# A two-layer trunk with a mixture of experts: conditioning's last four loads summed on PE, slots' weights taken from the transposed slot matrix, overflow tests at other pairs

## The chip, the cores and the metric

The kernel runs on one core of one Trainium2 chip. The metric is device time in microseconds (us) from start to end, as the median of several runs; beside it stands one execution with the hardware profiler, from which all rows are taken. Engines are named as in the profile: PE (TensorE) with its weight loads (PEld), DVE (VectorE), ACT (ScalarE), POOL (GpSimd), SP (SyncE, which only issues transfers here).

## What is computed

Two layers on 256 tokens with D = 1024, all in float32. A layer conditions its input with scale and shift vectors made from one vector c, mixes tokens by three branches (retention, attention with forget gates, latent attention) that are merged by gates and projected, then conditions again and runs a mixture of 32 experts: top-1 of four groups, then the two best experts of that group.

```python
for l in range(DEPTH):
    mod = silu(c) @ ada_w[l] + ada_b[l]              # 6 vectors of 1024: shift, scale, gate, twice
    h = modulate(rms_norm(x, norm1_g[l]), sh1, sc1)
    x = x + g1 * token_mixer(h, positions, ...)
    h = modulate(rms_norm(x, norm2_g[l]), sh2, sc2)
    x = x + g2 * hier_moe(h, ...)
return rms_norm(x, final_norm_g)

def hier_moe(h, w_grp, b_grp, w_exp, b_exp, w1, w3, w2):
    grp_p = softmax(t @ w_grp + b_grp);  g_idx = argmax(grp_p);  g_w = max(grp_p)
    exp_logits = (t @ w_exp + b_exp).reshape(T, 4, 8)
    top_p, top_i = top_k(softmax(exp_logits of g_idx), 2)
    wts = g_w[:, None] * top_p / sum(top_p)
    # each token goes to its two experts e with its weight w:
    y += w * ((silu(xb @ w1[e]) * (xb @ w3[e])) @ w2[e])
```

## The kernel before

**Tiles and stages.** Tokens are two tiles of 128 partitions (NT = 2); x stays on chip. A layer is `mixer(l)` and then `moe(l)`. Weights come from HBM as loads of 1 MiB (128 partitions, 2048 floats). `Ring.plan` lists all loads in the order in which they are wanted, and `Ring.fill` (L139) issues them in that order, all from SP, each as soon as a slot is free and its data may be overwritten. There are 12 slots of their own; in the MoE seven or so more places join, in tiles named `more_right`, `more_left` and `ar`. SP's queue goes in order: a load that waits for its slot holds up all loads behind it.

**Conditioning.** `ada()` takes loads of `ada_w`, two halves for each vector part. A load of a part in `vec` is summed by DVE in four operations (L511) into `acc`, and PE adds the sum of the partitions (`add_up` with `cz`). Any other load is summed by PE itself: four matmuls, each with 32 rows of output. `ga` is the generator that does one load per `next`; it is interleaved with the mixer. The last `ADA_TAIL` loads of a layer are planned behind the loads of the output projection. `ADA_FIRST` of them are taken in front of `route()`, any others in the MoE.

**From the mixer to the MoE.** `out()` multiplies by `out_w` in two halves of 512 columns, n = 0 and 1. After each half `residual` (L592, L593 on DVE, L594 on ACT, squares) updates x, and `router_half(n)` transposes x on PE (L188), copies the transposes by ACT (L1224) and multiplies them by the router's weights (matmuls with 36 columns). Then `route()` forms the inverse rms and runs `choose()` for both tiles, a chain of small DVE operations with, here and there, a `pulse`: one PE matmul on the operation's result, which nothing reads. It leaves `rr` (each token's place among its expert's tokens) and `W` (its weight) for each expert, both in the tile `rt`.

**The MoE.** The experts go in 16 pairs, numbered 0 to 15. An expert has CAP = 64 slots for tokens, so a pair has 128. For pair p: `up` of w1 into the bank G[0] (32 matmuls); `combine(p - 1)` adds the last pair's result to the tokens' sums (with OT, the transposed one-hots); silu on ACT (L1415); `slots_of(p)`; `up` of w3 into G[1]; the gather of the next pair's tokens (matmuls of x with one-hots made by DVE); hid transposed; w2; and the weighted results as two parts yh (L1454, ACT) and yl (L1455, DVE), scaled by `wsl`, the weight of each slot.

`slots_of(p)` makes one-hots on DVE (L1318), transposes them on PE, gets `wsl` by two matmuls of the one-hots with two columns of W, and copies both out of the bank:

```python
self.mm(ps[:, 256:258], oh[t], self.W[:, t, 2 * p:2 * p + 2], t == 0, t == 1)
...
nc.vector.tensor_copy(wsl(p)[es], ps[es, 256 + e:257 + e])        # L1372
nc.vector.tensor_copy(self.OT, ps[:, 0:256])                      # L1373
```

In front of pair OVERFLOW = 12 stands `overflow(l)`: a branch on whether any expert has more than 64 tokens (the rows show it not taken). `final_gain`, two matmuls and copies that spread the last norm's gain, stands at pairs 11 and 12 of the last layer.

Of the kernel before, what the change touches and what calls it, by code (L numbers as in the profile page):

```python
# [14 lines left out]
ALU = mybir.AluOpType  # L15
AX = mybir.AxisListType
# [4 lines left out]
NT = 2  # L21
DEPTH = 2
D_IN = 3524
NE = 32
CAP = 64
# [20 lines left out]
A_END = 9216  # L46


ADA_TAIL, ADA_FIRST = 2, 2

ADA_BEHIND = {2048: 1, 2560: 1, 0: 1}

# [4 lines left out]
WAIT_MLA, WAIT_FOX, WAIT_RET, WAIT_PT = 4, 4, 2, 1  # L57
SLOTS = 12

OVERFLOW = 12  # L60


def table(inputs):
# [102 lines left out]
class Trunk:  # L166
# [771 lines left out]
    def run(self, gen):  # L938
        for _ in gen:
            self.step(self.live)  # L940
# [84 lines left out]
    def mixer(self, l):  # L1025
        nc, run, finish = self.nc, self.run, self.finish
# [16 lines left out]
        def chain():  # L1043
            self.rowsA = yield from self.ada(l, 4, range(6), space, self.R, range(6))
            yield from self.gs(l, 1, 12 * l + 6, self.rowsA)
            yield from self.router_terms(l)
            while not self.y_free and gr not in self.live:
                yield
            yield from self.gate_rows(12 * l + 4, A_GT1, self.rowsA)
            self.gated = True  # L1050
            yield from later(0)
            self.rowsB = yield from self.ada(l, 10, range(2), lambda i: later(i + 1), self.v(A_RB, 512),
                                             range(min(2, inline // 2)))
            if l + 1 < DEPTH:
                rows = yield from self.ada(l + 1, 0, range(4), lambda i: later(i + 5 if i >= 0 else -1), self.acc[:, 1],
                                           range((inline - 4) // 2))
                yield from self.gs(l + 1, 0, 12 * l + 12, rows)
            self.parked = True

        ga = chain()  # L1060
# [104 lines left out]
        def out():  # L1165
            pa = [[self.bank("g") for _ in range(NT)] for _ in range(2)]
            for h in range(2):
                for n in range(2):
                    for j in range(4):
                        wh, wl = self.next_w()  # L1170
                        m = (self.yr[1], self.hr[0])[h][:, :, j]
                        for t in range(NT):
                            ts = slice(128 * t, 128 * t + 128)
                            self.mm3(pa[n][t], m[:, 0, ts], m[:, 1, ts], wh, wl, h + j == 0, h + j == 4)
                        yield
                    if h == 0:
                        continue
                    if n:
                        self.finish(half)
                    half = self.router_half(n)  # L1180
                    for t in range(NT):
                        self.residual(t, n, pa[n][t], self.v(A_RES + 512 * t, 512))
                        self.free(pa[n][t])
                        if n:
                            next(half)
                    if n:
                        self.together(half)
                    else:
                        self.live.append(half)
# [6 lines left out]
        while not self.gated:  # L1196
            self.step(self.live)
        run(out())
        while not self.parked:
            self.step(self.live)  # L1200
        pool = self.open_extra(l, "left", 3)
        parts = [pool.tile([P, 2, 512], F32R, name=f"{n}_{l}", tag=n) for n in ("yh", "yl")]
        self.yp = [[p[:, n] for p in parts] for n in range(2)]
        self.ring.grow([self.v(A_MORE[2], 2048)], l)
        self.tail = True
        for _ in range(ADA_FIRST):
            next(ga, None)
        self.route()
        self.rest = ga

# [33 lines left out]
    def choose(self, t, r):  # L1244
        nc = self.nc
        one = lambda: self.small(1)
        tt, tsc, red = nc.vector.tensor_tensor, nc.vector.tensor_scalar, nc.vector.tensor_reduce
        stt = nc.vector.scalar_tensor_tensor
        rt = self.v(A_RT + 132 * t, 132)
        lg, lm, o1, o2 = rt[:, 0:36], rt[:, 36:68], rt[:, 68:100], rt[:, 100:132]  # L1250
        stt(lg, self.psr[:, 64 * t:64 * t + 36], r, self.sb, ALU.mult, ALU.add)
        if t == NT - 1:
            self.free(self.psr)
        yield
        gmax, nmax, gsum, m2 = one(), one(), one(), one()
        g4 = lg[:, 0:4]
        c4, off = self.small(4), self.small(4)
        red(gmax, g4, AX.X, ALU.max)
        yield
        stt(c4, g4, gmax, self.desc, ALU.is_equal, ALU.mult)  # L1260
        self.pulse(t, c4)
        yield
        red(m2, c4, AX.X, ALU.max)
        self.pulse(t, m2)
        yield
        tsc(off, self.desc, m2, NEG, ALU.not_equal, ALU.mult)
        self.pulse(t, off)
        yield
        tt(lm.rearrange("p (g e) -> p g e", g=4), lg[:, 4:36].rearrange("p (g e) -> p g e", g=4),
           off[:, :, None].to_broadcast([P, 4, 8]), ALU.add)  # L1270
        yield
        top, idx, fi = self.small(8), self.small(8), self.small(2)
        nc.vector.max(top, lm)
        self.pulse(t, top)
        yield
        nc.vector.max_index(idx.bitcast(U32), top, lm)
        yield
        nc.vector.tensor_copy(fi, idx[:, 0:2].bitcast(U32))
        yield
        tsc(o1, self.iota0, fi[:, 0:1], None, ALU.is_equal)  # L1280
        self.pulse(t, o1)
        yield
        stt(self.mb[:, t], self.iota0, fi[:, 1:2], o1, ALU.is_equal, ALU.add)
        d, e2, den, w1, w2 = (one() for _ in range(5))
        ps = self.bank("s")
        if t == 1:
            self.mm(ps[:, 0:32], self.ones16, self.mb[:, 0], True, False)
        self.mm(ps[:, 0:32], self.sU, self.mb[:, t], t == 0, True)
        yield
        tsc(nmax, gmax, -1.0, None, ALU.mult)  # L1290
        tt(d, top[:, 1:2], top[:, 0:1], ALU.subtract)
        nc.scalar.activation(self.small(4), g4, AF.Exp, bias=nmax, accum_out=gsum)
        nc.scalar.activation(e2, d, AF.Exp)
        yield
        stt(self.rr[:, t], ps[:, 0:32], 1.0, self.mb[:, t], ALU.add, ALU.mult)
        self.free(ps)
        yield
        self.one_hot(0, t, r)
        tsc(o2, self.iota0, fi[:, 1:2], None, ALU.is_equal)
        yield  # L1300
        tsc(den, e2, 1.0, gsum, ALU.add, ALU.mult)
        yield
        nc.vector.reciprocal(w1, den)
        yield
        tt(w2, w1, e2, ALU.mult)
        tsc(self.W[:, t], o1, w1, None, ALU.mult)
        yield
        stt(self.W[:, t], o2, w2, self.W[:, t], ALU.mult, ALU.add)
        yield

    def one_hot(self, p, t, by=None):

        oh = self.v(A_OH[t] + 2 * CAP * (p % 2), 2 * CAP)
        for i in range(2):
            e = 2 * p + i
            o, r = oh[:, CAP * i:CAP * i + CAP], self.rr[:, t, e:e + 1]
            if by is None:
                self.nc.vector.tensor_scalar(o, self.iota1[:, 0:CAP], r, None, ALU.is_equal)  # L1318
            else:
                self.nc.vector.tensor_scalar(o, self.iota1[:, 0:CAP], r, by, ALU.is_equal, ALU.mult)  # L1320
        return oh


# [17 lines left out]
    def moe(self, l):  # L1341
        nc, tc = self.nc, self.tc
# [4 lines left out]
        wsl = lambda p: self.wsl[:, p % 2:p % 2 + 1]  # L1347
# [9 lines left out]

        def wanted(p):

            return [self.one_hot(p, t, self.rs[:, t:t + 1]) for t in range(NT)]  # L1360

        def slots_of(p):

            ps = S[2]
            oh = [self.one_hot(p, t) for t in range(NT)]
            for t in range(NT):
                self.tr(ps[:, 128 * t:128 * t + 128], oh[t])
            for t in range(NT):
                self.mm(ps[:, 256:258], oh[t], self.W[:, t, 2 * p:2 * p + 2], t == 0, t == 1)
            for e in range(2):  # L1370
                es = slice(64 * e, 64 * e + 64)
                nc.vector.tensor_copy(wsl(p)[es], ps[es, 256 + e:257 + e])  # L1372
            nc.vector.tensor_copy(self.OT, ps[:, 0:256])  # L1373

        def combine(p, halves=(0, 1)):

# [14 lines left out]

        self.together(self.gather([self.v(A_OH[t], 2 * CAP) for t in range(NT)], hg[0], True))
        for p in range(NE // 2):
            if p == OVERFLOW:
                combine(p - 1)
                self.overflow(l)
            hgT = hg[p % 2]
# [12 lines left out]
            up(G[0], "exp_w1")  # L1410
            if p == 0:
                self.together(self.rest)
            elif p != OVERFLOW:
                combine(p - 1)
            nc.scalar.activation(hid, G[0], AF.Silu)  # L1415
            slots_of(p)
            following = iter(()) if end else self.gather(wanted(p + 1), hg[(p + 1) % 2])
            up(G[1], "exp_w3")
            nc.vector.tensor_tensor(hid, hid, G[1], ALU.mult)  # L1419
            if l == DEPTH - 1 and OVERFLOW - 1 <= p <= OVERFLOW:  # L1420
                self.final_gain(p - (OVERFLOW - 1))
            if p == 0:
                R, vec = self.rowsB
                self.rowsB = self.acc[:R.shape[0], 1], vec
# [8 lines left out]
            ps = G[0]  # L1433
# [4 lines left out]
            for h, n0, nn in self.w2_parts(l, p):  # L1438
                sv = [self.ring.take((l, "exp_w2", 2 * p + e, h, n0)) for e in range(2)]
                for n in range(n0, n0 + nn):  # L1440
                    for i in range(2):
                        j = 2 * h + i
                        for e in range(2):
                            es = slice(64 * e, 64 * e + 64)
# [193 lines left out]
```

## Time and profile before

| | |
|---|---|
| median of 3 runs | 1554.18 us (1547.79, 1554.18, 1554.46) |
| profiled execution | 1548.13 us |
| its span, first to last instruction | 1546.5 us |
| mean granted clock of PE | 0.987 |
| PE busy | 1468.5 us (95%) |
| PEld busy | 897.6 us (58%) |
| DVE busy | 661.7 us (43%) |
| ACT busy | 447.9 us (29%) |
| read from HBM | 532.61 MB |

The profile is one execution. Busy times are shares of the span; a busy PE is one with a matmul under way, and matmuls are pipelined. The two MoE stretches, from some 330 us to 780 and from some 1080 to the end, are about six tenths of the span, and PE hardly pauses in them; the mixers ahead of them use all engines.

### The profile page before, as it was taken

To read this page: it belongs to the slowest core of one execution; us is meant where nothing else is said; L and a number is where in the kernel's file an instruction comes from. 1 tells how busy PE (TensorE), PEld (TensorE's weight loads), DVE (VectorE), ACT (ScalarE), POOL (GpSimd) and SP (SyncE) were. 2 spreads that over 40 slices of the span, in tenths; PEclk is the share of its full clock that TensorE was granted. 3 is DMA by queue.
4 is the path that set the end of the run, shared out by engine and by line. 5 is a ranking of instruction groups with operands and counts; after the bars stand their busy time and mean duration, and the time that the engine had idled before them with its cause. 6 is when DMAs were issued, how large, how long until landed. Compare 5 with 4: busy or idle time off the path is not lost. (4 is left out here: it accounts for less than half of the span.)

```text
span 1546.5 us, 21205 instructions
## 1 busy us (share of the span) xinstructions
PE 1468.5 (95%) x8326; PEld 897.6 (58%) x8326; DVE 661.7 (43%) x1756; ACT 447.9 (29%) x897; POOL 6.0 (0%) x10
## 2 busy tenths in 40 slices
PE   6898999999999999999989989999999999999996
PEld 3776889854444444444458679897444444444442
DVE  3766697962222222122157669767222222222223
ACT  3554534431111111111154454454211121111112
POOL 0000000000000000000000000000000000000001
PEclk9999999999999999999999999999999999999998
DMA  9963477998999999999995546668999999999993
GB/s 385 384 231 136 152 270 270 371 379 365 421 420 421 421 421 421 420 420 420 411 366 191 220 148 261 243 243 322 385 420 421 420 420 421 421 420 419 422 416 124
DMA packets 78542, 535.16 MB, mean 346 GB/s; under 512 B 8608, under 2 KB 8864, under 8 KB 15968
## 3 DMA queue, kind: packets, MB, share of 16 engines
q1 hardware_dynamic: 77776, 532.89, 85.2%
q8 instruction: 69, 1.13, 0.3%
q10 hardware_dynamic: 656, 0.80, 0.1%
q14 instruction: 41, 0.34, 0.1%
HBM read 532.61 MB, written 1.05 MB: 345 GB/s over the span
## 5 line engine op out<-in xcount | busy, mean ns | idle before, releaser
L179 PE MATMUL bank<-slot,ar 128*64 128x512 f32 (+1 forms) x1876 | 453.6, 593 | 1.8 <-ACT ar L1436 1.5
L179 PEld LDWEIGHTS bank<-slot,ar 128*64 128x64 f32 (+1 forms) x1876 | 143.0, 137 | 253.9 <-issue 235.6
L255 DVE TENSOR_TENSOR ws<-slot,ws 128x512 fp32r<-128x512 f32 (+1 forms) x276 | 186.5, 682 | 104.8 <-ACT ws L253 97.6
L179 PE MATMUL bank<-hr,ws 128*128 128x256 f32 x1536 | 204.7, 289 | 8.4 <-DVE ws L255 7.3
L179 PE MATMUL bank<-ar 128*64 128x512 f32 (+3 forms) x692 | 209.2, 502 | 0.7 <-DVE ar L885 0.7
L179 PEld LDWEIGHTS bank<-hr,ws 128*128 128x128 f32 x1536 | 191.8, 193 | 19.2 <-DVE ws L255 10.0
L253 ACT CAST ws<-slot 128x512 fp32r<-128x512 f32 (+1 forms) x276 | 164.4, 619 | 101.9 <-PE bank L179 95.8
L179 PE MATMUL bank<-ws,hr 128*128 128x512 f32 (+1 forms) x576 | 152.7, 410 | 10.0 <-ACT ws L253 4.6
L1338 ACT ACTIVATE ar<-bank,GS 128x128 f32<-128x128 f32 x128 | 58.6, 458 | 355.1 <-PE bank L179 324.3
L179 PE MATMUL bank<-more_left,ar 128*64 128x512 f32 x456 | 137.6, 594 | 0.0
L179 PEld LDWEIGHTS bank<-ar,x 128*128 128x128 f32 x1024 | 119.2, 192 | 25.1 <-issue 21.1
L179 PE MATMUL bank<-ar,x 128*128 128x128 f32 x1024 | 128.3, 278 | 1.7 <-DVE ar L1320 1.5
L179 PEld LDWEIGHTS bank<-ws,hr 128*128 128x128 f32 x576 | 107.7, 193 | 37.7 <-ACT ws L253 6.4
L1455 DVE SCALAR_TENSOR_TENSOR yl<-bank,wsl,yh 128x512 fp32r<-128x512 f32 x60 | 45.0, 750 | 157.6 <-ACT yh L1454 156.6
L179 PEld LDWEIGHTS bank<-ar 128*64 128x64 f32 (+2 forms) x692 | 80.9, 155 | 45.9 <-issue 38.1
L1372 DVE COPY wsl<-bank 64x1 f32<-64x1 f32 x64 | 10.0, 156 | 227.7 <-PE bank L179 227.2
L1336 DVE TENSOR_SCALAR ar<-bank,GS 128x128 f32<-128x128 f32 x128 | 52.5, 410 | 115.8 <-ACT ar L1338 115.8
L1419 DVE TENSOR_TENSOR R<-R,bank 128x512 f32<-128x512 f32 x32 | 22.0, 688 | 178.5 <-PE bank L179 178.5
L511 DVE SCALAR_TENSOR_TENSOR acc<-slot,cz,acc 128x512 f32<-128x512 f32 x122 | 90.8, 744 | 0.1
L179 PEld LDWEIGHTS bank<-more_left,ar 128*64 128x64 f32 x456 | 41.0, 137 | 82.5 <-issue 76.3
L1454 ACT ACTIVATE yh<-bank,wsl 128x512 fp32r<-128x512 f32 x60 | 41.3, 688 | 151.2 <-PE bank L179 151.2
L179 PE MATMUL bank<-yr,ws 128*128 128x256 f32 x576 | 75.4, 286 | 2.4 <-DVE ws L255 2.2
(244 smaller groups left out, 1158.8 us busy)
## 6 DMA issues: line engine op xcount, KB each, us to landing
slot<-in_exp_w SPq DMA_DIRECT2D x226, 1024.0 KB, 19.8
ar<-in_exp_w SPq DMA_DIRECT2D x54, 1024.0 KB, 19.8
more_left<-in_exp_w SPq DMA_DIRECT2D x54, 1024.0 KB, 19.8
slot<-in_ada_w SPq DMA_DIRECT2D x46, 1024.0 KB, 6.6
more_right<-in_exp_w SPq DMA_DIRECT2D x38, 1024.0 KB, 19.4
slot<-in_w_in SPq DMA_DIRECT2D x24, 1024.0 KB, 9.7
slot<-in_gate_w SPq DMA_DIRECT2D x23, 1024.0 KB, 5.0
slot<-in_branch_w SPq DMA_DIRECT2D x12, 1024.0 KB, 4.7
```

Of the source, the lines that this page charges most:

```text
L179: self.nc.tensor.matmul(out, lhsT, rhs, start=start, stop=stop, skip_group_check=True)
L253: self.nc.scalar.copy(hi, w)
L255: self.nc.vector.tensor_tensor(lo, w, hi.bitcast(F32), ALU.subtract)
L511: nc.vector.scalar_tensor_tensor(acc, v[:, t, :], c, acc, ALU.mult, ALU.add)
L1336: nc.vector.tensor_scalar(hgT[:, j], pv[:, i], G[:, j:j + 1], S[:, j:j + 1], ALU.mult, ALU.add)
L1338: nc.scalar.activation(hgT[:, j], pv[:, i], AF.Identity, bias=S[:, j:j + 1], scale=G[:, j:j + 1])
L1372: nc.vector.tensor_copy(wsl(p)[es], ps[es, 256 + e:257 + e])
L1419: nc.vector.tensor_tensor(hid, hid, G[1], ALU.mult)
L1454: nc.scalar.mul(self.yp[n][0], G[n], wsl(p))
L1455: nc.vector.scalar_tensor_tensor(self.yp[n][1], G[n], wsl(p), self.yp[n][0].bitcast(F32), ALU.mult, ALU.subtract)
```

## The change

Four edits. (1) `ADA_TAIL` and `ADA_FIRST` go from 2 to 4: the last four loads of conditioning per layer are planned behind the output projection's loads, and are all summed by PE; the place where they are taken moves from behind `out()` to between the end of the first half's `router_half` and the start of the second's. (2) One pulse in `choose` goes. (3) `one_hot` always has two operations, and `slots_of` makes its one-hots with each token's weight in the place of the one; their transposed matrix is summed along its row for `wsl` and compared with zero for `OT`, so that the matmuls with W and the copies go. (4) The overflow test moves from in front of the 13th pair to the 12th in layer 0 and the 14th in layer 1, and `final_gain` to pairs 13 and 14 of the last layer.

```diff
--- before.py
+++ after.py
@@ -46,7 +46,7 @@
 A_END = 9216
 
 
-ADA_TAIL, ADA_FIRST = 2, 2
+ADA_TAIL, ADA_FIRST = 4, 4
 
 ADA_BEHIND = {2048: 1, 2560: 1, 0: 1}
 
@@ -57,7 +57,7 @@
 WAIT_MLA, WAIT_FOX, WAIT_RET, WAIT_PT = 4, 4, 2, 1
 SLOTS = 12
 
-OVERFLOW = 12
+OVERFLOW = (11, 13)
 
 
 def table(inputs):
@@ -1177,6 +1177,11 @@
                         continue
                     if n:
                         self.finish(half)
+                        while not self.parked:
+                            self.step(self.live)
+                        self.tail = True
+                        for _ in range(ADA_FIRST):
+                            next(ga, None)
                     half = self.router_half(n)
                     for t in range(NT):
                         self.residual(t, n, pa[n][t], self.v(A_RES + 512 * t, 512))
@@ -1196,15 +1201,10 @@
         while not self.gated:
             self.step(self.live)
         run(out())
-        while not self.parked:
-            self.step(self.live)
         pool = self.open_extra(l, "left", 3)
         parts = [pool.tile([P, 2, 512], F32R, name=f"{n}_{l}", tag=n) for n in ("yh", "yl")]
         self.yp = [[p[:, n] for p in parts] for n in range(2)]
         self.ring.grow([self.v(A_MORE[2], 2048)], l)
-        self.tail = True
-        for _ in range(ADA_FIRST):
-            next(ga, None)
         self.route()
         self.rest = ga
 
@@ -1278,7 +1278,6 @@
         nc.vector.tensor_copy(fi, idx[:, 0:2].bitcast(U32))
         yield
         tsc(o1, self.iota0, fi[:, 0:1], None, ALU.is_equal)
-        self.pulse(t, o1)
         yield
         stt(self.mb[:, t], self.iota0, fi[:, 1:2], o1, ALU.is_equal, ALU.add)
         d, e2, den, w1, w2 = (one() for _ in range(5))
@@ -1295,7 +1294,7 @@
         stt(self.rr[:, t], ps[:, 0:32], 1.0, self.mb[:, t], ALU.add, ALU.mult)
         self.free(ps)
         yield
-        self.one_hot(0, t, r)
+        self.one_hot(0, t, lambda e: r)
         tsc(o2, self.iota0, fi[:, 1:2], None, ALU.is_equal)
         yield
         tsc(den, e2, 1.0, gsum, ALU.add, ALU.mult)
@@ -1308,16 +1307,13 @@
         stt(self.W[:, t], o2, w2, self.W[:, t], ALU.mult, ALU.add)
         yield
 
-    def one_hot(self, p, t, by=None):
+    def one_hot(self, p, t, by):
 
         oh = self.v(A_OH[t] + 2 * CAP * (p % 2), 2 * CAP)
         for i in range(2):
             e = 2 * p + i
             o, r = oh[:, CAP * i:CAP * i + CAP], self.rr[:, t, e:e + 1]
-            if by is None:
-                self.nc.vector.tensor_scalar(o, self.iota1[:, 0:CAP], r, None, ALU.is_equal)
-            else:
-                self.nc.vector.tensor_scalar(o, self.iota1[:, 0:CAP], r, by, ALU.is_equal, ALU.mult)
+            self.nc.vector.tensor_scalar(o, self.iota1[:, 0:CAP], r, by(e), ALU.is_equal, ALU.mult)
         return oh
 
 
@@ -1357,20 +1353,15 @@
 
         def wanted(p):
 
-            return [self.one_hot(p, t, self.rs[:, t:t + 1]) for t in range(NT)]
+            return [self.one_hot(p, t, lambda e: self.rs[:, t:t + 1]) for t in range(NT)]
 
         def slots_of(p):
 
             ps = S[2]
-            oh = [self.one_hot(p, t) for t in range(NT)]
             for t in range(NT):
-                self.tr(ps[:, 128 * t:128 * t + 128], oh[t])
-            for t in range(NT):
-                self.mm(ps[:, 256:258], oh[t], self.W[:, t, 2 * p:2 * p + 2], t == 0, t == 1)
-            for e in range(2):
-                es = slice(64 * e, 64 * e + 64)
-                nc.vector.tensor_copy(wsl(p)[es], ps[es, 256 + e:257 + e])
-            nc.vector.tensor_copy(self.OT, ps[:, 0:256])
+                self.tr(ps[:, 128 * t:128 * t + 128], self.one_hot(p, t, lambda e: self.W[:, t, e:e + 1]))
+            nc.vector.tensor_reduce(wsl(p), ps[:, 0:256], AX.X, ALU.add)
+            nc.vector.tensor_scalar(self.OT, ps[:, 0:256], 0.0, None, ALU.not_equal)
 
         def combine(p, halves=(0, 1)):
 
@@ -1391,7 +1382,7 @@
 
         self.together(self.gather([self.v(A_OH[t], 2 * CAP) for t in range(NT)], hg[0], True))
         for p in range(NE // 2):
-            if p == OVERFLOW:
+            if p == OVERFLOW[l]:
                 combine(p - 1)
                 self.overflow(l)
             hgT = hg[p % 2]
@@ -1410,15 +1401,15 @@
             up(G[0], "exp_w1")
             if p == 0:
                 self.together(self.rest)
-            elif p != OVERFLOW:
+            elif p != OVERFLOW[l]:
                 combine(p - 1)
             nc.scalar.activation(hid, G[0], AF.Silu)
             slots_of(p)
             following = iter(()) if end else self.gather(wanted(p + 1), hg[(p + 1) % 2])
             up(G[1], "exp_w3")
             nc.vector.tensor_tensor(hid, hid, G[1], ALU.mult)
-            if l == DEPTH - 1 and OVERFLOW - 1 <= p <= OVERFLOW:
-                self.final_gain(p - (OVERFLOW - 1))
+            if l == DEPTH - 1 and 0 <= p - OVERFLOW[l] <= 1:
+                self.final_gain(p - OVERFLOW[l])
             if p == 0:
                 R, vec = self.rowsB
                 self.rowsB = self.acc[:R.shape[0], 1], vec
```

How the orders of instructions move, at three places. First PE at the end of layer 1's mixer, as a difference (`cst,x` are transposes of x, `cst,ar` with 36 columns the router's, `cz` conditioning's loads from `ar` or a slot, `cst,sm` pulses):

```order
 L188 MATMUL bank_67<-cst,x 128x128 x4
 L179 MATMUL bank_69<-cst,ar 128x36 x8
+L179 MATMUL bank_70<-ar,cz 32x512 x8
+L179 MATMUL bank_70<-slot_92,cz 32x512 x4
+L179 MATMUL bank_70<-slot_90,cz 32x512 x4
 L188 MATMUL bank_64<-cst,x 128x128 x4
 L188 MATMUL bank_65<-cst,x 128x128 x4
 L179 MATMUL bank_69<-cst,ar 128x36 x8
-L179 MATMUL bank_70<-slot_92,cz 32x512 x4
-L179 MATMUL bank_70<-slot_89,cz 32x512 x4
 L179 MATMUL bank_63<-cst,sm 4x128
```

Four loads' matmuls (x8 are two loads, x4 one) stand ahead of the second half's transposes, where two stood behind its 36-column matmuls.

Then SP's queue at the same place. The loads are those of the first experts (`in_exp_w`); before:

```order
L139 DMA slot_98<-in_exp_w 128x2048
L139 DMA slot_100<-in_exp_w 128x2048
L139 DMA ar<-in_exp_w 128x2048 x2
L139 DMA more_left_7358<-in_exp_w 128x2048
L139 DMA more_left_7359<-in_exp_w 128x2048
L139 DMA more_left_7360<-in_exp_w 128x2048
L139 DMA ar<-in_exp_w 128x2048
L139 DMA slot_92<-in_exp_w 128x2048
L139 DMA slot_89<-in_exp_w 128x2048
```

and after, from the same place on:

```order
L139 DMA slot_99<-in_exp_w 128x2048
L139 DMA slot_95<-in_exp_w 128x2048
L139 DMA ar<-in_exp_w 128x2048 x2
L139 DMA slot_92<-in_exp_w 128x2048
L139 DMA slot_90<-in_exp_w 128x2048
L139 DMA more_left_7317<-in_exp_w 128x2048
L139 DMA more_left_7318<-in_exp_w 128x2048
L139 DMA more_left_7319<-in_exp_w 128x2048
L139 DMA ar<-in_exp_w 128x2048
L139 DMA slot_93<-in_exp_w 128x2048
```

Ahead of `more_left` stand now the four slots in which conditioning's last loads lie (`ar` twice, `slot_92`, `slot_90`); before, two of conditioning's slots (`slot_92`, `slot_89`) stood behind it.

Last DVE around the first `slots_of` of layer 1 (`rt` holds rr and W, `rs` the inverse rms); before:

```order
L556 SCALAR_TENSOR_TENSOR GS<-bank_68,cst 128x4
L555 COPY GS<-bank_68 128x4
L556 SCALAR_TENSOR_TENSOR GS<-bank_68,cst 128x4
L1318 TENSOR_SCALAR ar<-cst,rt 128x64 x4
L1372 COPY wsl<-bank_69 64x1 x2
L1373 CAST OT<-bank_69 128x256
L1320 TENSOR_SCALAR ar<-cst,rt,rs 128x64 x4
L1419 TENSOR_TENSOR R<-R,bank_64 128x512
```

and after:

```order
L556 SCALAR_TENSOR_TENSOR GS<-bank_68,cst 128x4
L555 COPY GS<-bank_68 128x4
L556 SCALAR_TENSOR_TENSOR GS<-bank_68,cst 128x4
L1316 TENSOR_SCALAR ar<-cst,rt 128x64 x4
L1363 TENSOR_REDUCE wsl<-bank_69 128x1
L1364 TENSOR_SCALAR OT<-bank_69 128x256
L1316 TENSOR_SCALAR ar<-cst,rt,rs 128x64 x4
L1410 TENSOR_TENSOR R<-R,bank_64 128x512
```

The two copies and the cast become a reduction and a comparison.

## Rows read from the trace of the kernel before

**Rows 1.** Windows, steady MoE: us, each engine's busy us, PEclk, DMA share, GB/s.
```profile
1300.00:1320.00 20.00, 20.00 (x96) 7.82 (x93) 4.05 (x14) 1.98 (x3) 0.00 (x0) 1.00 1.02 422
```
**Rows 2.** Timeline of ACT, silu: start, duration, instruction, idle time before and its releaser.
```profile
623.15 0.60 ACT L1415 ACTIVATE R<-bank 128x512 f32<-128x512 f32 x1 [6.26 <-PE bank L179]
651.01 0.60 ACT L1415 ACTIVATE R<-bank 128x512 f32<-128x512 f32 x1 [5.98 <-PE bank L179]
...
707.92 0.60 ACT L1415 ACTIVATE R<-bank 128x512 f32<-128x512 f32 x1 [6.26 <-PE bank L179]
```
**Rows 3.** Timeline of SP's queue, issues of pair 15's w1, layers 0 and 1.
```profile
736.76 0.33 SPq L139 DMA_DIRECT2D slot<-in_exp_w  x1
...
1479.39 2.82 SPq L139 DMA_DIRECT2D slot<-in_exp_w  x2
```
**Rows 4.** DMA issues at 736 to 737 and 1479 to 1480: KB each, us to landing.
```profile
slot<-in_exp_w SPq DMA_DIRECT2D x1, 1024.0 KB, 19.8
...
slot<-in_exp_w SPq DMA_DIRECT2D x1, 1024.0 KB, 20.3
```
**Rows 5.** Timeline of PE, w1 of pair 15, layers 0 and 1.
```profile
755.96 7.60 PE L179 MATMUL bank<-slot,ar 128*64 128x512 f32 x33
...
1497.54 10.61 PE L179 MATMUL bank<-slot,ar 128*64 128x512 f32 x48
```
**Rows 6.** Timeline of PE in one pair, the matmuls with W and the next.
```profile
1395.63 0.51 PE L179 MATMUL bank<-rt,ar 128*128 128x2 f32 x4
1396.06 0.64 PE L179 MATMUL bank<-more_left,ar 128*64 128x512 f32 x1
```
**Rows 7.** Timeline of DVE in one pair, the cast and the gather's one-hots.
```profile
683.06 0.42 DVE L1373 CAST OT<-bank 128x256 fp32r<-128x256 f32 x1
683.41 0.97 DVE L1320 TENSOR_SCALAR ar<-cst,rt,rs 128x64 f32<-128x64 f32 x4
```
**Rows 8.** Timeline of PE, from layer 0's mixer to its route.
```profile
316.50 0.98 PE L179 MATMUL bank<-cst,ar 128*128 128x36 f32 x8
317.73 1.04 PE L179 MATMUL bank<-acc,cz 128*32 128x512 f32 x2 [0.25 <-DVE acc L511]
...
319.62 1.42 PE L188 MATMUL bank<-cst,x 128*128 128x128 f32 x8
...
323.04 1.07 PE L179 MATMUL bank<-ar,cz 128*32 128x512 f32 x8
323.92 1.04 PE L179 MATMUL bank<-slot,cz 128*32 128x512 f32 x8
```
**Rows 9.** Timeline of PE, layer 1: a sum in the mixer, then to the route.
```profile
1011.75 1.05 PE L179 MATMUL bank<-acc,cz 128*32 128x512 f32 x2
...
1066.78 1.92 PE L179 MATMUL bank<-cst,ar 128*128 128x36 f32 x16
1068.53 1.07 PE L188 MATMUL bank<-cst,x 128*128 128x128 f32 x8
...
1071.95 1.93 PE L179 MATMUL bank<-slot,cz 128*32 128x512 f32 x16
1073.69 1.04 PE L179 MATMUL bank<-cst,sm 128*4 128x128 f32 x8
```
**Rows 10.** Windows in pair 0 of layer 0, columns as in rows 1.
```profile
361.00:363.00 2.00, 2.00 (x12) 0.69 (x10) 0.00 (x0) 0.00 (x0) 0.00 (x0) 1.00 0.15 49
342.00:344.00 2.00, 2.00 (x8) 1.33 (x9) 0.76 (x5) 0.00 (x0) 0.00 (x0) 0.50 1.01 422
```
**Rows 11.** Timeline of SP's queue, layer 1, around the route and pair 0.
```profile
1064.71 2.64 SPq L139 DMA_DIRECT2D more_left<-in_exp_w  x3
...
1084.22 0.80 SPq L139 DMA_DIRECT2D slot<-in_exp_w  x2
...
1104.61 0.80 SPq L139 DMA_DIRECT2D more_right<-in_exp_w  x2
```
**Rows 12.** Timeline of PE, first half of w3 in pair 0 of layer 0.
```profile
343.19 6.15 PE L179 MATMUL bank<-more_right,ar 128*64 128x512 f32 x16
```

## The prediction

> **What bounds the kernel now.** I read the MoE first: most of the time lies there, and two of the change's edits run once per pair of experts. The windows view of a steady 20 us [rows 1] shows two resources full at once: PE is busy all the time at a granted clock of 1.00, and the DMA share is 1.02 at 422 GB/s. Which of them sets the pace decides what an edit on PE is worth. ACT's timeline tells [rows 2]: silu (L1415), once per pair, always starts behind PE, 27.86 us after the one before (651.01 − 623.15). A pair's weights are 12 loads of 1 MiB; at 422 GB/s one takes 1.048576 / 0.422 = 2.49 us, and twelve 29.9 us. So DMA is slower than PE by 2.0 us per pair, yet PE does not wait: it lives on loads that were stored ahead in slots before the MoE began, and the lead shrinks from pair to pair. What is left of it at the end tells how much PE could gain.
>
> Follow one load to its use in the last pair. In layer 0 the second half of pair 15's w1 is issued at 736.76 [rows 3] and lands 19.8 us later [rows 4], at 756.56. PE's row of 33 [rows 5] begins with one matmul of the pair before, some 0.5 us; 16 for the first half take 3.5 us (10.61 / 48 × 16), so the second half starts at 759.95: 3.4 us to spare. In layer 1 the same load is issued at 1479.39, lands 20.3 us later at 1499.7, and feeds the third group of 16 in the row of 48 that starts at 1497.54, at 1504.6: 4.9 us to spare. So PE is the bound, with 3.4 and 4.9 us of slack on DMA's side, in a profiled execution of 1548.13 us.
>
> **The change, part by part.**
>
> *Slots' weights (32 pairs).* Two matmuls of 128x2 (four rows) leave PE. They start at 1395.63 and the next matmul at 1396.06 [rows 6]: 0.43 us, times 32 = 13.8 us of PE. DVE loses two copies of 64x1 and a cast of 128x256, and gets a sum over 256 columns and a comparison of 128x256, neither of which the trace shows. The nearest row is that cast at 0.42 us [rows 7], and I take 0.42 for each; from below nothing, from above three times the cast, 2.5 us for both. Either lies beside w3, 32 matmuls or some 7 us of PE, since the bank that they read is wanted next by the following pair's gather, behind w3: cost 0, and it would begin to cost from some 6 us on. The one-hots get a second operation, as the form that takes 0.97 us for four [rows 7]; DVE waits while w1 runs, so 0 again.
>
> *Conditioning.* Two more loads per layer go from DVE to PE. A load is four matmuls, eight rows: 323.92 − 323.04 = 0.88 us [rows 8], or two in 1073.69 − 1071.95 = 1.74 [rows 9]. Four take 3.48 us. They stand now between the 36-column matmuls of the first half and the transposes of the second, on PE's way to the route. Layer 0: the transposes start at 319.62 now, after the 36-column matmuls in two parts and a sum of acc for which PE waits 0.25 us for DVE. After: 316.50, 1.75 for all the 36-column matmuls (1066.78 to 1068.53 in layer 1), 3.48 for the loads, 321.73: **+2.1 us**. Layer 1: 3.48 later than 1068.53, while one sum of acc (1.05 us at 1011.75) leaves PE earlier in the mixer: **+2.4 us**. The two loads that stood behind the transposes are no gain there: the route waits for ACT's squares and DVE's chain, which start behind the same transposes. If they did hold it, their 1.74 us come back, so from below it is +0.4 and +0.7.
>
> *The pulse* is one matmul that nothing waits for: 0. *The overflow test* costs (707.92 − 651.01) − 2 × 27.86 = 1.19 us [rows 2] wherever it stands: 0, within ±1.2.
>
> *What is late next: the loads.* In layer 0 DMA idles at 361 to 363 us, share 0.15 [rows 10], for slots that pair 0's w2 frees. That point comes 2.1 − 0.43 = **1.7 us** later, and all loads from there on, since DMA does not pause again. In layer 1 SP's queue goes in order. Before, three loads into more_left are issued at 1064.71 [rows 11]; now the conditioning's four slots stand ahead of them, and the first is free at 1068.53 − 1.05 + 0.88 = 1068.4. By the order 16 loads follow up to the one that was issued at 1104.61: 16 × 2.49 = 39.8 us, to 1108.2, without a pause, since the slots issued at 1084.22 come free at 1086.6, while 8 loads (19.9 us) keep DMA busy to 1088.3. So **+3.6 us**; from below it is PE's own 2.4.
>
> *The sum.* At a layer's end the later of two decides. Layer 0: PE alone would be at 2.1 − 15 × 0.43 = −4.4, the load allows 1.7 − 3.4 = −1.7, then pair 15's own −0.43: −2.1. Layer 1: PE −4.0, the load 3.6 − 4.9 = −1.3, then −0.43: −1.7. Together −3.8 us, so 1548.13 − 3.8 = **1544.3 us**. Most of the 13.8 us turns into waits for loads in pairs 14 and 15. The profiled execution lies 6.05 us below the median of the runs shown (1554.18); on that the same sum gives 1550.4. The runs spread over 6.7 us, so I name the middle, **1547.3 us**.
>
> [...] In the same window PEld is busy for 7.82 of 20 us, 0.39, beside DMA's 1.02 [rows 1]. [...]
>
> **The rivals.**
>
> *DMA keeps up (0.15).* If the order of slots gives the delays back or loads run a little quicker, PE's gain stays whole: −13.8 + 2.1 + 2.4 = −9.3, **1538.8 us**. For it: 19.8 and 20.3 us from issue to landing are eight loads of 2.49, so there are slots free that far ahead. Against it: the share is 1.02 without a gap, so an early issue lands no earlier.
>
> *DMA is the bound in most runs: slower (0.2).* Two of the three runs are 6 us above the profiled one. Some 156 loads (13 pairs) from the gap to pair 15 take 388 us; a DMA slower by 0.9% eats 3.4 us, by 1.3% 4.9 us. Then what PE saves per pair buys nothing, and the later start of the loads is paid in full: 1.7 + 3.6 = +5.3, **1553.4 us** (1559.5 on the median). It turns against the kernel when the two delays exceed what is left of the slack plus the last pairs' 2 × 0.43; in the profile that is 3.4 + 4.9 + 0.9 = 9.2 against 5.3.
>
> *The clock (0.15).* [...]
>
> *The change does not do what it says:* for the overflow test that is the forecast itself, 1.19 us moved from one pair to another. For the weights the order shows the matmuls gone.
>
> **How the numbers follow.** The forecast has 0.5. A measurement of this kernel can tell some 0.5% (7.7 us) from no change. Of the forecast 0.12 lie faster than that, 0.37 within, 0.01 slower; of DMA that keeps up 0.11 and 0.04; of DMA as the bound 0.13 within and 0.07 slower; of the clock 0.05, 0.09 and 0.01. That makes faster 0.28, same 0.63, slower 0.09. The range starts at 1540, just above the first rival on the profiled time, and ends at 1558, just below the second on the median; it leaves out half of each and holds all the others.
>
> **What the profile after would show.** Silu every 27.43 us until loads limit it. Waits of PE for DMA, none in the middle pairs, and 2 to 3 us in pairs 14 and 15 of each layer; if they come by pair 8 the second rival holds, if there are none the first. The second half's transposes 5.2 us behind the first 36-column matmul. The loads into more_left issued behind four slots that wait for the conditioning's matmuls, and a gap of DMA in layer 1 that lasts until some 1068. A period longer by 1.2 us at the 12th and at the 14th pair. I would be wrong if PE waited for DVE's sum ahead of the gather, or if the route hung on the conditioning's matmuls otherwise than by 2.1 and 2.4 us.

## The result: slower by 0.65%

The changed kernel takes 1560.6 us (median of 8 runs, 1559.84 to 1565.68), the kernel before 1551.57 us in the runs beside it (8 runs). The ratio is 1.0065, with a 95% interval of 1.0049 to 1.0081. The runs of one kernel fall into two heaps some 6 us apart (1547.6 to 1549.4 and 1553.7 to 1554.5 for the kernel before), so medians of a few runs can differ by more than the ratios, which are all to the kernel before in runs beside. The prediction had 1547.3 us, a range of 1540 to 1558, and 0.09 for slower. The profiled execution took 1560.31 us with a span of 1558.7 us, 12.2 us more than before.

The page shows less work and more time: PE is busy for 3.1 us less than in the table of before and waits more.

```profile
PE 1465.4 (94%) x8222; PEld 886.9 (57%) x8222; DVE 660.5 (42%) x1708; ACT 447.8 (29%) x897; POOL 5.9 (0%) x10
...
q8 instruction: 68, 1.11, 0.3%
```

The timeline of ACT with silu (L1406 now) tells where, as it did before [rows 2]:

```profile
621.38 0.60 ACT L1406 ACTIVATE R<-bank 128x512 f32<-128x512 f32 x1 [6.26 <-PE bank L179]
...
660.29 0.60 ACT L1406 ACTIVATE R<-bank 128x512 f32<-128x512 f32 x1 [17.38 <-PE bank L179]
...
685.91 0.60 ACT L1406 ACTIVATE R<-bank 128x512 f32<-128x512 f32 x1 [6.26 <-PE bank L179]
...
713.42 0.60 ACT L1406 ACTIVATE R<-bank 128x512 f32<-128x512 f32 x1 [6.26 <-PE bank L179]
```

A pair takes 713.42 − 685.91 = 27.51 us, 0.345 less than before. But the pair with the overflow test costs (685.91 − 621.38) − 2 × 27.51 = 9.51 us where it had cost 1.19: 8.3 us more. In layer 1 the same sum over three pairs, with `final_gain` in both kernels, gives 11.5 us against 3.2. Together that is 16.7 us more than before, and more than all else gains. What PE does there is in its timeline:

```profile
644.09 0.40 PE L179 MATMUL bank<-yh,OT 128*128 128x512 f32 x1
644.33 0.40 PE L179 MATMUL bank<-yl,OT 128*128 128x512 f32 x1
650.79 6.00 PE L179 MATMUL bank<-slot,ar 128*64 128x512 f32 x16 [6.06 <-PEq L1473]
```

PE stands still for 6.06 us behind its own sequencer (PEq) at L1473, the `tc.If` of `overflow(l)`, and the next 16 rows (eight float32 matmuls) take 6.00 us instead of 3.54 (a third of 10.61 [rows 5], at a granted clock of 1.00). The instructions of that line (durations in ns, shortest, median, longest, then first and last start) show the branch itself, in the changed kernel:

```profile
L1473 ACTq COMPARE_BRANCH  x2: 45/50/54, 642.8 to 1447.5; - x2
...
L1473 DVEq COMPARE_BRANCH  x2: 63/68/72, 643.6 to 1448.3; - x2
...
L1473 PEldq COMPARE_BRANCH  x2: 6100/6114/6128, 644.3 to 1449.1; - x2
```

and in the kernel before (L1482 there):

```profile
L1482 PEldq COMPARE_BRANCH  x2: 446/454/462, 674.0 to 1417.5; - x2
```

The same jump over the same code took 0.45 us and takes 6.11, on PE alone. The windows (columns as in rows 1) show the second half of the price, a granted clock of 0.50 behind the pause:

```profile
644.00:650.00 6.00, 0.73 (x3) 0.23 (x2) 0.98 (x4) 0.00 (x0) 0.00 (x0) 0.89 1.02 415
650.00:653.00 3.00, 2.21 (x6) 0.85 (x8) 0.00 (x0) 0.00 (x0) 0.00 (x0) 0.50 1.00 418
```

So a test costs 6.1 − 0.45 = 5.7 us of standing and 6.00 − 3.54 = 2.5 us of slow matmuls, 8.2 of the 8.3 us seen.

### The profile page after: what moved, and what is told of

Read it like the earlier page. It is cut to its first block, busy times and chain, and to the rows that moved or that the text cites. A ratio compares the mean times of both kernels' runs of the same rounds, so it can differ in the third digit from the quotient of the medians.

```text
span 1558.7 us, 20939 instructions
## 1 busy us (share of the span) xinstructions
PE 1465.4 (94%) x8222; PEld 886.9 (57%) x8222; DVE 660.5 (42%) x1708; ACT 447.8 (29%) x897; POOL 5.9 (0%) x10
## 3 DMA queue, kind: packets, MB, share of 16 engines
q8 instruction: 68, 1.11, 0.3%
## 5 line engine op out<-in xcount | busy, mean ns | idle before, releaser
L179 PE MATMUL bank<-slot,ar 128*64 128x512 f32 (+1 forms) x1888 | 459.2, 596 | 7.5 <-PEq L1473 6.1
L255 DVE TENSOR_TENSOR ws<-slot,ws 128x512 fp32r<-128x512 f32 (+1 forms) x284 | 191.7, 683 | 113.5 <-ACT ws L253 104.3
L253 ACT CAST ws<-slot 128x512 fp32r<-128x512 f32 (+1 forms) x284 | 169.3, 619 | 105.2 <-PE bank L179 95.3
L179 PE MATMUL bank<-more_left,ar 128*64 128x512 f32 x448 | 134.1, 610 | 5.9 <-PEq L1473 5.9
L179 PEld LDWEIGHTS bank<-ar,x 128*128 128x128 f32 x1024 | 124.2, 198 | 24.8 <-issue 21.1
L179 PE MATMUL bank<-ar,x 128*128 128x128 f32 x1024 | 133.0, 285 | 1.5 <-DVE ar L1316 1.5
L1363 DVE TENSOR_REDUCE wsl<-bank 128x1 f32<-128x256 f32 x32 | 13.6, 425 | 226.8 <-PE bank L188 226.8
L1406 ACT ACTIVATE R<-bank 128x512 f32<-128x512 f32 x32 | 19.2, 599 | 214.4 <-PE bank L179 214.4
L511 DVE SCALAR_TENSOR_TENSOR acc<-slot,cz,acc 128x512 f32<-128x512 f32 x108 | 80.4, 745 | 0.0
```

The costliest lines, as they stand in the source:

```text
L179: self.nc.tensor.matmul(out, lhsT, rhs, start=start, stop=stop, skip_group_check=True)
L253: self.nc.scalar.copy(hi, w)
L255: self.nc.vector.tensor_tensor(lo, w, hi.bitcast(F32), ALU.subtract)
L511: nc.vector.scalar_tensor_tensor(acc, v[:, t, :], c, acc, ALU.mult, ALU.add)
L1363: nc.vector.tensor_reduce(wsl(p), ps[:, 0:256], AX.X, ALU.add)
```

## The experiments

**What could make a branch long.** The test's code is skipped; PE jumps over 438 instructions of its own. Counted in the program's order, with a float32 matmul as four instructions (two rows, each with its weight load) and any other as two, PE's program has some 17,440 instructions in the changed kernel. The page's queue q8 has 68 packets with 1.11 MB: 16.3 KB each, and 17,440 / 68 = 256 instructions. That PE's program comes in blocks of 256 is the author's estimate from these two numbers. Counted from the program's start, the two branches of the kernel before stand 203 and 208 instructions behind a multiple of 256, those of the changed kernel at 100 and 60, since 8 instructions per pair went, conditioning's were added, and the tests moved. Theory A: whether a jump is short hangs on where the branch stands in its block. Theory B: an edit ahead of the branch makes it long (DVE's new operations, the absent matmuls). Theory C, the prediction's own second rival: the later loads cost the time.

*1. Other places for the tests.*

```diff
-OVERFLOW = (11, 13)
+OVERFLOW = (6, 9)
```

> The changed kernel, with the overflow tests in front of the 7th pair in layer 0 and the 10th in layer 1, nothing else. Theory A (where PE's branch lies in its program): PE's program comes in blocks of 256 instructions; with a float32 matmul as four instructions and any other as two, the branches of the kernel before stand 203 and 208 instructions behind a multiple of 256 and took 0.45 us, those of the changed kernel stand at 100 and 60 and took 6.1 us. Here they stand at 201 and 192, so both take 0.45 us again, the clock stays at 1.00 behind them, some 2 x 8 us go, and loads begin to limit in the last pairs: 1544 to 1546 us. Theory B (the branch is long because of an edit ahead of it, the weights by DVE or the missing matmuls): 6.1 us in both again, 1560 us. Theory C (the later loads cost the time): 1555 us or more.

It took 1556.53 us, ratio 1.0038 [1.0022, 1.0055]. The branch at 201 was short, that at 192 long:

```profile
L1473 PEldq COMPARE_BRANCH  x2: 450/3295/6140, 512.4 to 1338.2; - x2
```

Half a miss: 192 was thought to be inside. Two branches of one program differ, 9 instructions apart in their blocks; B has no reason for that.

*2. The same places, with PE's program shifted by 104 instructions.*

```diff
             R = self.v(A_NB, 512)
+            for _ in range(26):
+                self.mm(self.S[2][0:8, 0:8], self.cz[:, 0, 24:32], self.cz[:, 0, 24:32], True, True)
```

> The changed kernel with its tests where they are, and 26 float32 matmuls of 8x8 on zeros added at the start, while PE waits for its first loads: 104 instructions, so that the branches stand at 204 and 164 behind a multiple of 256. Theory A: layer 0's branch falls to 0.45 us; layer 1's at 164 is outside of what was seen to be short (203, 208), and by where the fetches fall I expect it long, 6.1 us. The time falls by one stall, to 1551 to 1553 us. Theory B: both stay at 6.1 us, 1560 us.

1554.69 us, ratio 1.0036 [1.0015, 1.0056]: one stall less. Layer 0's branch, at 204, went from 6.13 to 0.45 us; layer 1's, at 164, stayed long.

```profile
L1473 PEldq COMPARE_BRANCH  x2: 450/3234/6018, 645.5 to 1443.5; - x2
```

*3. The kernel before with the fourth edit alone* (`OVERFLOW = (11, 13)` and `final_gain` with it).

> The kernel before with the fourth edit alone: tests in front of the 12th pair in layer 0 and the 14th in layer 1, final_gain with it. The branches stand at 164 and 243. Theory A: 164 long (6.1 us) as in the run with the filler, 243 short (0.45 us); the time is 7 to 9 us above the kernel before. If both are long it is 14 to 17 us, if both are short 0 +- 1.2. Theory B: both short, no change.

1562.85 us, ratio 1.0091 [1.0062, 1.0119]. Layer 0's branch at 164 took 6.26 us, layer 1's at 243 0.43 us, as A said. Moving the tests, without any other edit, costs as much as the whole change. That is above the 7 to 9 us expected. In the profile (14.4 us longer) layer 0's test is 9.0, 2.2 go with a pause behind layer 1's branch at 243 (see run 5), 2.2 came up in layer 1's mixer, which no edit touches (last section), and 1.2 ahead of the first silu.

*4. The kernel before with the third edit alone* (slots' weights), tests in front of the 13th pair.

> The kernel before with the third edit alone: slots' weights from the transposed matrix, tests in front of the 13th pair as before. The pairs are 8 instructions shorter, so the branches stand at 107 and 240. Theory A: layer 0's takes 6.1 us and brings the lower clock, layer 1's 0.45; silu comes every 27.5 us. Layer 0 ends 3 us later than before, layer 1 gains 5 us up to the loads' slack: -2.5 us, 1545 to 1549. Theory B with DVE's new operations as the cause: both at 6.1 us, 1554 or more. That loads set the pace (the rival of the prediction): silu stays at 27.86 us, 1556.

1548.33 us, ratio 0.9989 [0.9973, 1.0005]. The branch at 107 took 6.24 us, the one at 240 0.44. Silu came every 27.51 us up to pair 11: loads don't set the pace, so C falls. DVE's new operations are there and layer 1's branch is short, while run 3 has none of the edits that B blames and a long one: B falls. Layer 1's pair with the test costs 2.0 us more than before in spite of its short branch (see run 5).

*5. The changed kernel with both branches inside* (`OVERFLOW = (7, 10)`).

> The changed kernel with tests in front of the 8th pair in layer 0 and the 11th in layer 1; the branches stand at 232 and 223 behind a multiple of 256, both inside what was short so far (201 to 243). Theory A: both 0.45 us, no fall of the clock behind them, and the whole 16 us back: 1543 to 1546 us, where what is left is the weights' gain against the route's loss, and loads that begin to limit at pair 15. Theory B (places themselves cost, wherever PE's program lies): one or both long again, 1552 or 1560 us.

1546.2 us, ratio 0.998 [0.9961, 0.9999]: some 13 to 14 us below the changed kernel. Both branches took 0.42 to 0.46 us. But the pair with layer 0's test still cost 3.1 us, not 1.2. PE's timeline shows a second, smaller pause 36 instructions (18 rows and their weight loads) behind the branch:

```profile
540.98 3.65 PE L179 MATMUL bank<-more_right,ar 128*64 128x512 f32 x16 [0.40 <-PEq L1473]
544.43 1.02 PE L179 MATMUL bank<-slot,ar 128*64 128x512 f32 x2
546.30 3.65 PE L179 MATMUL bank<-slot,ar 128*64 128x512 f32 x14 [0.85 <-issue]
```

PE goes on at 546.30, 6.1 us behind the start of the branch (540.2), as long as a long branch takes; that this is the same wait, met some rows later, is the author's reading. Run 8's branch in layer 0 stands later in its block, at 240 against 232 here, and has fewer rows behind it and a longer pause: 1.90 us behind 14 rows against 0.85 behind 18, again until 6.2 us behind the branch (542.2):

```profile
542.87 3.62 PE L179 MATMUL bank<-more_right,ar 128*64 128x512 f32 x14 [0.40 <-PEq L1475]
548.38 0.59 PE L179 MATMUL bank<-more_right,ar 128*64 128x512 f32 x1 [1.90 <-issue]
```

*6. The third edit alone, with both branches inside* (208 and 240).

```diff
-OVERFLOW = 12
+OVERFLOW = (7, 12)
```

> The kernel before with the third edit alone, and layer 0's test moved to the 8th pair so that the branches stand at 208 and 240. Both short. PE alone would gain 32 x 0.345 = 11 us; loads allow some 3.4 + 4.9 + 0.7 = 9 us: 1539 to 1541 us on runs like the profiled one of before, 8 to 10 us below the kernel before, with waits of PE for DMA in pair 15. If loads set the pace all along (the prediction's second rival), no gain.

1542.83 us, ratio 0.9951 [0.9933, 0.9968], so about 1542 against 1549.3, slightly above the 1539 to 1541 expected. The gain is some 7.5 us of 11. Of the rest, 2.0 us go with the pause behind layer 1's branch at 240 (1.35 us of standing in the timeline), and loads hold up pair 15 of layer 0, as the prediction had it for the changed kernel:

```profile
756.32 3.65 PE L179 MATMUL bank<-slot,ar 128*64 128x512 f32 x14 [0.30 <-DMA slot<-in_exp_w]
```

The line shows 0.30 us of it; silu comes 28.86 us after the one before instead of 27.51, so the wait is 1.35 us in all. Layer 1 does not wait for loads.

*7. The first edit alone* (conditioning), pulse kept, branches at 231 and 222.

> The kernel before with the first edit alone (conditioning's four loads on PE ahead of the second half), the pulse kept, and layer 1's test in front of the 12th pair so that both branches are short (231 and 222). Theory: the route 2.3 and 1.8 us later as in the changed kernel, the first gather slower by 2.0 and 2.6 us at the lower clock, pair 0 of layer 0 quicker by 2.6 us: 5 to 7 us above the kernel before. If the clock in the first gather hangs on the pulse that the change took away, only 1 to 4 us above, with the gather at 4.2 us.

1558.51 us, ratio 1.0046 [1.0031, 1.0061], 7 us by the ratio. The first gather took 6.12 us in layer 0 and 6.49 in layer 1 with the pulse in place, so the pulse is not what kept it at 4.21. The first edit is a loss by itself; 1.6 us of the 7 go with the small pause of run 5, at 231 in layer 0. Pair 0 of layer 0 took 30.63 us from silu to silu with the matmuls with W in place, and 33.4 in runs 4, 6 and 10, where they are gone.

*8. PE's idle time in the route filled* (on top of run 5).

```diff
+        for _ in range(2):
+            self.mm(self.G[0], self.ident, self.cst[:, 0:512], True, True)
         self.route()
```

> The changed kernel with tests as in the run with both branches short, and two float32 matmuls of 128x512 on constants added in front of the route's chain, where PE has nothing to do for 1.25 and 0.65 us. Theory: it is this idle time that brings the lower clock; with 1.7 us of it filled the first gather takes 4.2 us instead of 6.1 and 6.8, PE is 2.0 and 2.6 us earlier, and the time falls by 1 to 4 us against the run without them, less where loads then limit. Rival: the clock falls anyway, and nothing changes.

1550.74 us, ratio 1.0 [0.9979, 1.002]: no gain over run 5, rather a loss. In layer 1 the theory held: the granted clock was 1.00 (1086 to 1090 us; 0.50 at 1082 to 1086 in run 5) and the first gather took 4.21 us, not the 6.79 of the changed kernel:

```profile
1085.67 4.21 PE L179 MATMUL bank<-ar,x 128*128 128x128 f32 x32 [0.76 <-DVE ar L1318]
```

In layer 0 it failed: the wait was filled as well, but the gather took 5.83 us (granted clock 0.65 at 336 to 340 us), and the lower clock came back in pair 0 (0.50 at 352 to 356 us, 1.00 there in run 5; 33.25 us from silu to silu against 30.53). The 8 and 16 instructions moved the branches to 240 and 239, with the pause shown above, and the pairs with tests cost 2.5 us more than in run 5. What the clock gave in layer 1 (2.5 us), these took twice over. So work in the place of the wait kept the clock up in layer 1 alone; for layer 0 the cause stays open.

*9. Tests where the change put them, both branches inside* (run 2's filler, and 11 such matmuls between the layers).

```diff
             for l in range(DEPTH):
+                for _ in range(11 * l):
+                    self.mm(self.S[2][0:8, 0:8], self.cz[:, 0, 24:32], self.cz[:, 0, 24:32], True, True)
                 self.mixer(l)
```

> The changed kernel with its tests where they are (12th and 14th pair), the 26 float32 matmuls of 8x8 at the start, and 11 more between the layers: the branches stand at 204 and 208, as in the kernel before. Theory A, with what the runs with branches at 231 to 240 added (0.8 to 1.9 us in which PE has nothing to issue some 30 instructions behind the branch): both branches take 0.45 us, nothing is waited for behind them, the pairs with tests cost 1.2 us, the time is 1543 to 1546 us, 15 us below the changed kernel with 37 matmuls more. Rival (place and length of PE's program have nothing to do with it): 1560 us.

1546.18 us, ratio 0.9988 [0.9971, 1.0004]: 14.4 us below the changed kernel by the medians, 14.7 by the spans of the profiled executions (1558.7 and 1544.0), with 37 matmuls more and nothing else changed.

```profile
L1473 PEldq COMPARE_BRANCH  x2: 433/439/445, 644.4 to 1442.1; - x2
```

```profile
621.42 0.60 ACT L1406 ACTIVATE R<-bank 128x512 f32<-128x512 f32 x1 [6.26 <-PE bank L179]
...
652.28 0.60 ACT L1406 ACTIVATE R<-bank 128x512 f32<-128x512 f32 x1 [9.33 <-PE bank L179]
...
677.92 0.60 ACT L1406 ACTIVATE R<-bank 128x512 f32<-128x512 f32 x1 [6.26 <-PE bank L179]
```

The test costs (677.92 − 621.42) − 2 × 27.51 = 1.48 us at the 12th pair, where it had cost 9.51. That settles it for A.

*10. Run 6 with layer 1's branch at 205* (`OVERFLOW = (7, 11)`).

> The kernel before with the third edit alone and tests in front of the 8th pair in layer 0 and the 12th in layer 1: branches at 208 and 205. Theory: both 0.45 us and no wait behind them; against the run with 208 and 240 layer 1 is 1 to 1.9 us shorter, less what its loads then hold up in pair 15; layer 0 waits there for its loads by 1.4 us as in that run. 1540 to 1542 us, the fastest of all.

1542.82 us, ratio 0.9956 [0.994, 0.9973]: not told apart from run 6, where 1 to 1.9 us less was expected. In the profile layer 1 is 1.95 us shorter from its first silu to its last (415.42 us against 417.37), as expected, but the first silu of layer 0 came 1.1 us later than in run 6's profile, and pair 15 of layer 0 waits 1.37 us for its loads as there (silu after 28.88 us); a difference of this size is lost in the spread of the runs (1538.04 to 1546.05). Runs 6 and 10 are faster than both kernels.

All 24 branches, by position in the block of 256 (us): 60 6.10; 100 6.13; 107 6.24; 164 6.02 and 6.26; 192 6.14; 201 to 208 0.43 to 0.46 (nine of them); 222 to 243 0.37 to 0.46 (nine). Between 192 and 201 lies the border; positions from 244 on to 59 were not tried.

The small pauses give the same border in another way. From a branch to where PE goes on are 441 instructions (the 438 and three of the test itself), and each row behind it is two; the pauses in layer 0 (18, 19 and 14 rows behind branches at 232, 231 and 240) then stand at 709 to 710, that is 2 × 256 + 197 or 198, those in layer 1 (15 rows behind 243; 17 behind 240, 240 and 239) at 202 or 203; the five between the layers are not explained. The pauses of layer 0 thus lie at 197 or 198 behind a multiple of 256, between 192 and 201 as the border does. That blocks begin thereabouts in this count, and not at its multiples of 256, is the author's estimate from these numbers.

Queue q8 ("instruction") shows the packets themselves. One packet starts 3.5 to 3.9 us behind each of the 24 branches, long or short (3.8 and 3.6 us in the kernel before, 3.7 and 3.6 in the changed kernel). Ahead of them they differ: the last packet before started 3.3 to 5.8 us ahead of each of the 18 short branches (3.8 and 3.7 us in the kernel before), and 11.6 us or more ahead of the six long ones (17.1 and 11.65 us in the changed kernel). That a long branch waits for the packet behind it is the author's reading; the traces of the changed kernel show the packet's start, 3.6 to 3.7 us behind the branch's, and the branch's end, 6.1 us behind it.

## Why the prediction was wrong

**The step that failed** is "the overflow test costs 1.19 us wherever it stands: 0, within ±1.2". It took a measured price of one branch at one position of the program for the price of any such branch. The rows showed 1.19 us and no reason for it; nothing of before showed what the branch would cost at another place. It was off by 8.3 and 8.4 us, and by itself moves the forecast of 1544.3 to 1561. The same holds for "the change does not do what it says": that rival was put down as the forecast itself.

**Slots' weights:** right, with a size that was off. 0.43 us per pair was forecast, 27.86 − 27.515 = 0.345 measured, 11.0 us instead of 13.8. DVE's new operations cost nothing, since silu still waits for PE alone; the sum takes 425 ns, as was taken from the cast. The page has it (busy us, mean ns, idle before):

```profile
L1363 DVE TENSOR_REDUCE wsl<-bank 128x1 f32<-128x256 f32 x32 | 13.6, 425 | 226.8 <-PE bank L188 226.8
```

**Conditioning:** right in layer 0's route, and short of the clock behind it. PE's timeline after:

```profile
316.58 1.92 PE L179 MATMUL bank<-cst,ar 128*128 128x36 f32 x16
318.44 1.93 PE L179 MATMUL bank<-slot,cz 128*32 128x512 f32 x16
320.18 1.04 PE L179 MATMUL bank<-ar,cz 128*32 128x512 f32 x8
321.04 1.04 PE L179 MATMUL bank<-slot,cz 128*32 128x512 f32 x8
322.01 1.09 PE L188 MATMUL bank<-cst,x 128*128 128x128 f32 x8
...
326.77 1.38 PE L179 MATMUL bank<-cst,sm 128*4 128x128 f32 x8 [1.25 <-DVE sm L1260]
...
329.91 6.20 PE L179 MATMUL bank<-ar,x 128*128 128x128 f32 x32 [0.75 <-DVE ar L1316]
```

The transposes stand 322.01 − 316.58 = 5.43 us behind the first 36-column matmul (5.2 forecast), and 2.4 later than in [rows 8]. In layer 1 the same distance grew by 3.7 us (5.43 against 1.75 in [rows 9]), and what lies ahead, from layer 0's last silu on, had gained 2.0, so the gather starts some 1.8 later, for 2.4 forecast.

**The clock:** the prediction gives it 0.15, a chance for which no row of before and no run gives a figure; the runs showed a fall in one place and none in another. With the loads gone from between, PE waits 1.25 us for DVE in the route, and the granted clock is 0.50 in the gather, in both layers, where layer 1's had 1.00 in the kernel before (1076.5 to 1080.7 us). In pair 0 of layer 0 it stays at 1.00, where the kernel before has 0.50 [rows 10] and 6.15 us for 16 rows [rows 12] that take 3.65 here. That the matmuls with W are gone is not the cause: run 7 has them and took 30.63 us for the pair, runs 4, 6 and 10 lack them and took 33.4. The windows of the changed kernel:

```profile
330.00:333.00 3.00, 3.00 (x13) 2.91 (x14) 1.97 (x14) 1.20 (x7) 0.00 (x0) 0.50 1.01 429
...
1080.00:1084.00 4.00, 3.08 (x15) 1.91 (x14) 3.73 (x31) 1.83 (x5) 0.00 (x0) 0.50 1.01 426
...
345.00:348.00 3.00, 2.12 (x13) 1.15 (x14) 2.06 (x10) 0.62 (x1) 0.00 (x0) 1.00 1.02 418
```

The gather takes 6.20 and 6.79 us instead of 4.21, +2.0 and +2.6; pair 0 takes 30.52 us instead of 33.57, −2.7 beside the 0.35 of the weights. The prediction's sum has no term for the gathers or for pair 0, and the pulse that the change takes away is not the cause of the slower gathers (6.12 and 6.49 us with the pulse in place, run 7).

**Loads late in pairs 14 and 15:** not seen in the changed kernel, since PE itself came 8 us late to each end. With layer 0's branch short it came in pair 15 of layer 0 alone, and with 0.8 to 1.7 us (runs 1, 2, 6, 9 and 10) instead of 2 to 3; in runs 5 and 8, where the small pause holds PE back, it did not.

**The sum over the changed kernel:** +16.7 for the tests, +2.3 and +1.8 to the first gathers, +2.0 and +2.6 in them, −2.7 in pair 0, −10.4 for 30 pairs between the first silu and the last of each layer (the pair between is in the 1.8): +12.3, where 12.4 is measured up to the last silu and 12.2 up to the end. Without the tests it is −4.4; the forecast was −3.8, and run 9 with both branches short has 1546.18 us for 1547.3 forecast. That these lie so near is in part luck: the weights gave less than forecast, the first gathers lost 4.6 us and pair 0 won 2.7, and the loads, which were to take most of the gain, took nothing in the changed kernel and 1.0 us in run 9. Of the rivals with loads, DMA as the bound is refuted by the period in runs 4, 6 and 9; DMA that keeps up is refuted by the waits in layer 0's pair 15, but holds in layer 1, where there are none.

## What to carry to other kernels

In this case the price of a skipped branch depended on where it stands in PE's program: 0.45 us, 0.45 and a pause of up to 1.9 us soon after, or 6.1 us plus 2.5 us at a granted clock of 0.50, from the same code. An edit that does no more than change the number of PE's instructions ahead of it flipped it (run 2: 26 small matmuls, 6.13 to 0.45 us); look at the branch's own duration in the profile before a difference is put down to the edit, count instructions to the branch, and set its place last. A stall that is priced from one row should have its cause named, or the range should hold its other value.

## What the runs showed of the hardware

- Queue q8 of the changed kernel moved 68 packets with 1.11 MB, 16.3 KB each; one for 256 of PE's 17,440 instructions is the author's estimate. The packet behind layer 0's long branch stands in the DMA view at 647 to 648 us (packets, MB, share), 3.7 us behind the branch's start at 644.3; the branch ends 6.1 us behind its start:

```profile
q8 instruction: 1, 0.02, 6.7%
```

- The pause behind a short branch late in the short stretch (0.85 and 1.00 us at 232 and 231, 1.35 to 1.90 us at 239 to 243, none from 201 to 208) was not expected; it shows as "issue", without a releaser, and ends 6.1 to 6.4 us behind the start of the branch, wherever it begins.
- A step of 5.5 to 6 us arises in the first 80 us in the profiled executions of runs 1, 4, 5, 7 and 8: the first gather starts at 336.03 us in run 5's and at 329.98 in run 9's, though the code up to there differs by 26 small matmuls alone. Part of it is the clock: the 21 matmul rows at 51.48 us of run 5's profile take 7.39 us at a granted clock of 0.52 (51 to 58 us), the same rows at 49.28 of run 9's 4.92 us at 1.00. Shifts of 1 to 2 us arise likewise in layer 1's mixer (2.2 us in run 3). What brings it about stays open.
